# Hybrid mLSTM / latent-attention encoder layer: weight buffers that change roles, projection operands built during attention, an earlier last column

## Chip, cores and metric

One core of one Trainium2 chip runs the whole program in one launch. The metric is the device time of one execution in microseconds (us). The median of three runs of the kernel before is 1942.12 us (1938.83 to 1942.77).

## What is computed

One encoder layer is applied to two token groups of 512 tokens (`x_prompt`, `x_sample`; width 1024) with shared fp32 weights:

```python
u = h @ w_in                                   # h = rmsnorm(x); q,k,v,o, gates, c_q, c_kv, k_r, gm
hm = rmsnorm(mlstm(q, k, v, log_i, log_f))     # both directions, 4 heads
y_m = (sigmoid(o) * hm) @ w_mo
y_a = mla_attention(q_nope, q_rope, k_nope, k_rope, va) @ w_ao     # 8 heads
g_m, g_a = split(sigmoid(gm), 2)
x = x + (g_m * y_m + g_a * y_a) @ w_out
h2 = rmsnorm(x)
x = x + (silu(h2 @ w_gate) * (h2 @ w_up)) @ w_down                 # 2816 wide
x = x + sigmoid(x @ w_ple_gate) * (p @ w_ple)
y = rmsnorm(x)
```

## The kernel before

**Tiles and precision.** Activations are kept feature-major: a tile is 128 features by the 512 tokens of one group g. Every operand of a product is split into a high and a low fp32r part: a cast on ScalarE (ACT) makes the high part (`xh`, `wp`, `whi`), a subtraction on VectorE (DVE) the low part (`xl`, `wp`, `wlo`), and three matmuls hi·hi, hi·lo, lo·hi accumulate in PSUM.

**Order of the work.** A scheduler orders the instructions of each engine; the stretches between `pinned[0] = True` and `pinned[0] = False` (embedding projection, last column and tail) keep the program's order. All DMAs are issued in order by one queue engine (SP); a DMA waits there for its buffer to be free, and all later ones behind it. The stages, with their place in the profiled execution:

| stage | us | code |
|---|---|---|
| mLSTM, 4 heads | 30 to 600 | `mlstm_proj` (L464), `mlstm_chain` (L529) |
| attention, 8 heads, 16 half-heads (head `hd`, group g) | 600 to 871 | loop at L950 |
| merged projections `w_mo`, then `w_ao` | 871 to 1031 | `Seven`, `chain` (L840, L891) |
| output projection, embedding projection `emb` | 1031 to 1166 | L1076 |
| feed-forward gate and up, 22 units | 1166 to 1600 | `Seven`, `chain` |
| down projection | 1590 to 1830 | `Seven`, `chain` |
| ple gate, final norm, outputs | 1830 to 1938 | L1286 to L1299 |

**Seven products.** `Seven` computes a 2x2 block product (two groups, two blocks of weight columns) with seven products instead of eight, as in Strassen's scheme. One unit needs the four weight blocks a11, a12, a21, a22, which come in two loads of 512 KB: the first (a11|a12) into a buffer `wst` of pool WP, the second (a21|a22) into a buffer `wst` of pool WX; each pool has two such buffers. POOL adds and subtracts weight blocks in place, ACT and DVE split them into `wp` tiles (`wsplit`), PE multiplies. `chain` interleaves units: the order is P6(i), P1(i+1), P5(i), P2(i+1), Q4(i), P7(i+1), P3(i). So a11 and a12 are needed first (P1, P2) and come free last (P3, split in the last place), and a21, a22 come free two products earlier (Q4).

**Activation operands.** `Ops` builds the seven operands of each of the four feature blocks k from four tiles a, b (group 0 and 1, block k) and c, d (block k + 4): P1 = a, P2 = c, P3 = d, P7 = b − d, P6 = P7 − a, P5 = a − b, Q4 = P6 + c. Each is split into an `xh`/`xl` pair in pool H (P1, P2, P7, P6: 32 tiles) or OP. For `w_mo` the tiles come from the DRAM scratch `hzd`, which `mlstm_chain` wrote (L602 to L603: (tanh + 1)·hm). `hraw` loads a tile into X2, a pool opened at head 7, and multiplies it by the head-norm gain `hg` on ACT. All of P1, P2, P7 (`hops.need`) is asked for at head 7, ahead of that head's two half-heads; P6 comes with `chain`'s look-ahead.

**Embedding and tail.** `emb` (L1076) splits the weights `wple` in the step that uses them first. At the end, `finish` writes normalised output columns of a half of group 1 on DVE, `embed` computes the last embedding column with its squares, `sums` and `inv` the norm.

All instructions of the kernel before are recorded through one wrapper, so every row of its profile has line L77; groups are told apart by the tiles' names. Names in what follows: `ld` a loaded activation tile, `t` a difference of such tiles, `hn` a normalised activation tile, `sc`, `p`, `pt`, `aph`/`apl`, `av` the scores, probabilities, their transposes, their split and the attention output, `b` the PSUM bank of a `Seven` product, `mm` one of the other projections, `actd` the DRAM copies of feed-forward activations.

## Time and profile before

| quantity | value |
|---|---|
| median of 3 runs | 1942.12 us |
| profiled execution, its own time | 1939.74 us |
| span of the profiled execution | 1938.0 us |
| PE busy | 1861.9 us (96%), 8836 instructions |
| DVE busy | 1260.3 us (65%), 2135 instructions |
| ACT busy | 874.7 us (45%), 1711 instructions |
| POOL busy | 474.4 us (24%), 349 instructions |
| mean granted TensorE clock | 0.981 |

PE is TensorE's matmul stream. Busy time of PE holds the waits inside a running chain of matmuls only in part, so a stretch is better judged by its count of matmuls against the count of a stretch that is known to be full. "Granted clock" is 1.00 at 2.4 GHz and 0.50 at 1.2 GHz.

### The profile page before, as it was taken

The numbers are of one execution on the slowest core, as the hardware profiler recorded it, in microseconds if no ns is written. First come the engines' busy times: TensorE is split into PE (matmuls) and PEld (weight loads), VectorE is DVE, ScalarE is ACT, GpSimd is POOL, SyncE is SP. The second block draws the span as 40 slices with busy tenths as digits, with TensorE's granted clock in tenths as the row PEclk, the third lists the DMA queues.
The fourth block names the chain that finished last, engine by engine and source line by source line (L and its number), as shares of the span: only waits on it lengthen the run. The fifth ranks groups of instructions, "written<-read, shape, count | busy, mean of one in ns | idle before, by whom it ended". The sixth has DMA issues, their size and how long they took to land. (4 is left out here: it accounts for less than half of the span.)

```text
span 1938.0 us, 24531 instructions
## 1 busy us (share of the span) xinstructions
PE 1861.9 (96%) x8836; PEld 1542.6 (80%) x8836; DVE 1260.3 (65%) x2135; ACT 874.7 (45%) x1711; POOL 474.4 (24%) x349
## 2 busy tenths in 40 slices
PE   7999999999999999979899989999999999999997
PEld 6888898988888888758777867777887777788886
DVE  7657575746455676878996667445444458778757
ACT  5245454535354566784533435233333344434442
POOL 3000000100000001234630014565466654232100
PEclk9999999999999999989999989999999999999998
DMA  4110112012262122137554331233223346534232
GB/s 161 50 44 33 55 35 64 34 60 82 82 202 90 55 74 73 53 115 239 163 200 153 109 114 66 87 111 106 94 97 102 115 135 218 163 120 142 87 125 87
DMA packets 95578, 203.40 MB, mean 105 GB/s; under 512 B 10400, under 2 KB 21024, under 8 KB 95456
## 3 DMA queue, kind: packets, MB, share of 16 engines
q1 hardware_dynamic: 95456, 201.83, 31.2%
q8 instruction: 69, 1.13, 0.2%
q14 instruction: 53, 0.43, 0.1%
HBM read 147.69 MB, written 54.10 MB: 104 GB/s over the span
## 5 line engine op out<-in xcount | busy, mean ns | idle before, releaser
L77 PE MATMUL b<-xh,wp 128*128 128x512 f32 x2296 | 723.4, 396 | 17.9 <-ACT wp L77 8.3
L77 PEld LDWEIGHTS b<-xh,wp 128*128 128x128 f32 x2296 | 434.5, 190 | 124.4 <-ACT wp L77 11.7
L77 PE MATMUL b<-xl,wp 128*128 128x512 f32 x1148 | 452.4, 394 | 5.9 <-DVE xl L77 5.7
L77 DVE TENSOR_TENSOR wp<-wst,wp 128x512 fp32r<-128x512 f32 (+1 forms) x284 | 271.9, 964 | 108.8 <-ACT wp L77 108.0
L77 ACT CAST wp<-wst 128x512 fp32r<-128x512 f32 (+1 forms) x284 | 171.0, 611 | 345.4 <-PE b L77 228.1
L77 PEld LDWEIGHTS b<-xl,wp 128*128 128x128 f32 x1148 | 217.8, 190 | 54.3 <-DVE xl L77 7.6
L77 PE MATMUL mm<-hh,whi 128*128 128x512 f32 x592 | 233.1, 394 | 7.2 <-ACT whi L77 7.0
L77 PE MATMUL mm<-hh,wlo 128*128 128x512 f32 x592 | 232.4, 394 | 2.2 <-DVE wlo L77 2.2
L77 PE MATMUL mm<-hl,whi 128*128 128x512 f32 x592 | 233.0, 394 | 1.1 <-DVE hl L77 1.1
L77 POOL TENSOR_TENSOR s<-wst,wst 128x512 f32<-128x512 f32 (+1 forms) x42 | 61.6, 1466 | 449.5 <-DMA wst<-w 323.4
L77 PEld LDWEIGHTS mm<-hh,whi 128*128 128x128 f32 x592 | 112.2, 190 | 30.6 <-ACT whi L77 7.0
L77 POOL TENSOR_TENSOR wst<-wst 128x512 f32<-128x512 f32 (+1 forms) x84 | 125.7, 1496 | 35.3 <-DVE wp L77 30.7
L77 PEld LDWEIGHTS mm<-hh,wlo 128*128 128x128 f32 x592 | 112.1, 189 | 26.1 <-DVE wlo L77 3.4
L77 PEld LDWEIGHTS mm<-hl,whi 128*128 128x128 f32 x592 | 112.1, 189 | 25.5 <-DVE hl L77 2.3
L77 DVE TENSOR_TENSOR u<-b,u 128x512 f32<-128x512 f32 x90 | 61.3, 687 | 107.6 <-PE b L77 82.7
L77 ACT CAST whi<-wst 128x1024 fp32r<-128x1024 f32 (+1 forms) x71 | 73.1, 1029 | 110.4 <-PE mm L77 77.6
L77 DVE TENSOR_TENSOR wlo<-wst,whi 128x1024 fp32r<-128x1024 f32 (+1 forms) x71 | 86.0, 1211 | 28.7 <-ACT whi L77 28.3
L77 POOL TENSOR_TENSOR vnl<-avt,vnh 128x512 fp32r<-128x512 f32 x16 | 21.5, 1345 | 317.6 <-ACT vnh L77 284.6
L77 DVE TENSOR_TENSOR xl<-ld,xh 128x512 fp32r<-128x512 f32 x109 | 88.7, 846 | 8.1 <-ACT xh L77 7.8
L77 PE MATMUL mm<-xh,wp 128*128 128x512 f32 (+1 forms) x288 | 81.7, 368 | 0.0
L77 ACT COPY u<-b 128x512 f32<-128x512 f32 x90 | 50.9, 586 | 66.6 <-PE b L77 65.6
L77 DVE TENSOR_TENSOR x<-x,b 128x512 f32<-128x512 f32 x84 | 56.9, 682 | 32.8 <-PE b L77 32.4
(269 smaller groups left out, 3379.4 us busy)
## 6 DMA issues: line engine op xcount, KB each, us to landing
wst<-w SPq DMA_DIRECT2D x135, 512.0 KB
ld<-actd SPq DMA_DIRECT2D x77, 256.0 KB
actd<-t SPq DMA_DIRECT2D x44, 256.0 KB
actd<-sg SPq DMA_DIRECT2D x33, 256.0 KB
x<-x SPq DMA_DIRECT2D x32, 256.0 KB
wst<-wd SPq DMA_DIRECT2D x16, 512.0 KB
hzd<-hz SPq DMA_DIRECT2D x16, 256.0 KB
tmd<-tg SPq DMA_DIRECT2D x16, 256.0 KB
```

Source lines behind the costliest of these rows:

```text
L77: r = f(*args, **kw)
```

## The change

Five edits, each with its own place:

- **A.** `mlstm_proj` multiplies and shifts the tanh tile by `hg` on ACT (`hg`·tanh + `hg`, 16 more ACT instructions of 128x512), so that `hzd` already holds the gained product; in the chain the DVE operation is a plain product. The 16 multiplications by `hg` in `hraw` go.
- **B.** The 16 units of operands P1, P2, P7, P6 of `w_mo` are asked for in the six half-heads (4,0) to (6,1), 3, 3, 3, 3, 2 and 2 units each (`HOPS`). Their tiles pass through four staging buffers (two `rs` of H, two `bk` of EV), and P7 and P6 are made in place of b. At head 7 the 16 tiles are loaded a second time into X2 for P5, Q4, P3; there Q4 = (c − a') − d with a' = a − b takes two subtractions on POOL for each block instead of one addition.
- **C.** `Seven` gives the first load a WP buffer and the second a WX buffer in two units, and the other way round in the next two.
- **D.** `emb` splits the weights of the next step one step ahead.
- **E.** The last `embed` and its sums of squares (now without the DVE addition, in eight instead of four small matmuls) go ahead of outputs 2 and 3, and outputs 4 to 7 are spread among the norm's steps.

```diff
@@ mlstm_proj
                 S.activation(out=to[g][c], in_=to[g][c], func=AF.Tanh, scale=0.5)
+                hc = hg[:, 2 * hd + c : 2 * hd + c + 1]
+                S.activation(out=to[g][c], in_=to[g][c], func=AF.Identity, scale=hc, bias=hc)
@@ mlstm_chain
-            V.scalar_tensor_tensor(out=zt, in0=to[g][c], scalar=1.0, in1=tp, op0=ALU.add, op1=ALU.mult)
+            V.tensor_tensor(out=zt, in0=to[g][c], in1=tp, op=ALU.mult)
@@ Ops.part
             if name == "P7":
-                t = self.t[k] = self.tmp()
+                t = self.t[k] = self.tmp() or self.get("b", k)
...
-            else:
+            elif k in self.t:
                 t = self.t[k]
                 add(out=t, in0=t, in1=self.get("c", k), op=ALU.add)
+            else:
+                t = self.get("c", k)
+                add(out=t, in0=t, in1=self.get("a", k), op=ALU.subtract)
+                add(out=t, in0=t, in1=self.get("d", k), op=ALU.subtract)
@@ Seven
-            for sl, src in zip((WP, WX), srcs):
+            for sl, src in zip((WP, WX) if wsn[0] % 4 < 2 else (WX, WP), srcs):
...
+            wsn[0] += 1
@@
+    stage = [(H, "rs"), (H, "rs"), (EV, "bk"), (EV, "bk")]
+    raws = [0]
+
     def hraw(g, k):
-        t = load(hzd[g][k], X2, "x")
-        S.activation(out=t, in_=t, func=AF.Copy, scale=hg[:, k : k + 1])
-        return t
-
-    tmps = [(H, "rs"), (H, "rs"), (EV, "bk"), (EV, "bk")]
-    hops = Ops(hraw, lambda: (lambda s: s[0](s[1], "t"))(tmps.pop(0)), lambda n: V if n == "P7" else GP)
+        raws[0] += 1
+        return load(hzd[g][k], *stage[raws[0] % 4])
+
+    hops = Ops(hraw, None, lambda n: V if n == "P7" else GP)
+    hops.tmp = lambda: None
+    units = [(n, [k]) for k in range(4) for n in ("P1", "P2", "P7", "P6")]
@@ attention loop
             X2 = Slots("X2", "right", x=16)
-            for n in ("P1", "P2", "P7"):
-                hops.need(n)
+            hops.r, hops.t = {}, {}
+            hops.raw = lambda g, k: load(hzd[g][k], X2, "x")
         for g in range(G):
             attn(hd, g, ops[g])
             if hd < AH - 1:
                 ops[g] = attn_proj(hd + 1, g, wa)
+            for _ in range(HOPS.get((hd, g), 0)):
+                hops.need(*units.pop(0))
@@ emb
-            if c // 2 == len(wple):
+            while len(wple) < min(4, c // 2 + 2):
@@ tail
-    finish(1, [0, 1, 2, 3], 0, H0)
-    embed(KD - 1, 1, bk[3], toks[1], bps[1])
+    first = rs2[1]
+    finish(1, [0, 1], 0, H0)
+    embed(KD - 1, 1, bk[3], toks[1], bps[1], True)
+    finish(1, [2, 3], 0, H0)
     sums(1, H0, H0)
     inv(1, H0)
-    rs_ = rs2[1]
+    finish(1, [4, 5], 0, H0)
     spread3(1, H0, H0)
...
+HOPS = {(4, 0): 3, (4, 1): 3, (5, 0): 3, (5, 1): 3, (6, 0): 2, (6, 1): 2}
```

**Where instructions move.** First, the DMA issues of SP in the feed-forward stage, for one unit: `wst` is a weight load (the lower number is the first, a11|a12), `actd<-t` a store of an activation. Before:

```order
L849 DMA wst_13171<-w 128x1024
L1134 DMA actd_13030<-t_13014 128x512
L1134 DMA actd_13026<-t_13015 128x512
L849 DMA wst_13169<-w 128x1024
L1134 DMA actd_13028<-t_13016 128x512
L1134 DMA actd_13032<-t_13017 128x512
```

and now:

```order
L855 DMA wst_13201<-w 128x1024
L1150 DMA actd_13062<-t_13046 128x512
L1150 DMA actd_13058<-t_13047 128x512
L855 DMA wst_13203<-w 128x1024
L1150 DMA actd_13060<-t_13048 128x512
L1150 DMA actd_13064<-t_13049 128x512
```

Before, the second load (13171) stood ahead of the first (13169); now the first (13201) stands ahead, in the place that comes free with Q4 of an earlier unit, and the second (13203) behind it.

Second, VectorE in attention around half-head (4,0): `mx` rows are steps of the softmax, `apl` is the low part of the transposed probabilities, `qnl` of a query, `wp_8554` a weight of the merged projection's first unit. Before:

```order
L77 RECIPROCAL mx_7378<-mx_7378 128x1
L77 TENSOR_SCALAR mx_7398<-mx_7398 128x1
L77 TENSOR_TENSOR apl_7331<-pt_7365,aph_7330 128x4x128
L77 TENSOR_REDUCE mx_7464<-sc_7458 128x1
L77 RECIPROCAL mx_7398<-mx_7398 128x1
L77 TENSOR_TENSOR qnl_7437<-pj_7428,qnh_7435 128x512
L77 TENSOR_SCALAR mx_7464<-mx_7464 128x1
L77 TENSOR_TENSOR wp_8554<-s_1510_8551,wp_8554 128x512
L77 TENSOR_REDUCE mx_7484<-sc_7478 128x1
```

and now:

```order
L152 TENSOR_TENSOR xl_7622<-ld_7484,xh_7620 128x512
L152 TENSOR_TENSOR xl_7628<-ld_7624,xh_7626 128x512
L752 RECIPROCAL mx_7394<-mx_7394 128x1
L152 TENSOR_TENSOR xl_7634<-ld_7630,xh_7632 128x512
L752 RECIPROCAL mx_7414<-mx_7414 128x1
L748 TENSOR_REDUCE mx_7501<-sc_7495 128x1
L152 TENSOR_TENSOR qnl_7453<-pj_7444,qnh_7451 128x512
L748 TENSOR_REDUCE mx_7521<-sc_7515 128x1
L805 TENSOR_TENSOR ld_7789<-ld_7789,ld_7791 128x512
```

Before, all `xl` rows of these operands stood in and behind head 7. Now all 16 pairs and the four P7 subtractions (20 DVE rows) lie between the softmax rows of half-heads (3,1) and (5,0); (6,1), (7,0) and (7,1) have none. `ld_7789` takes the staging buffer of `ld_7484`, whose last reader on DVE is the first row, eight rows ahead.

Third, VectorE at the end of the embedding projection, where the normalised tiles `hn` and the operands `xl` of the feed-forward stage are made. Before:

```order
L77 TENSOR_TENSOR wp_10725<-wst_10560,wp_10725 128x512
L77 SCALAR_TENSOR_TENSOR hn_10748<-x_1855_10275,cols,rbc_10720 128x512
L77 SCALAR_TENSOR_TENSOR hn_10750<-x_1912_10493,cols,rbc_10720 128x512
L77 TENSOR_TENSOR wp_11000<-wst_10974,wp_11000 128x512
L77 TENSOR_TENSOR t_10762<-hn_10748,hn_10750 128x512
L77 TENSOR_TENSOR xl_10766<-t_10762,xh_10764 128x512
L77 SCALAR_TENSOR_TENSOR hn_10778<-x_1870_10334,cols,rbc_10720 128x512
L77 SCALAR_TENSOR_TENSOR hn_10780<-x_1924_10542,cols,rbc_10720 128x512
L77 TENSOR_TENSOR t_10762<-t_10762,hn_10377 128x512
L77 TENSOR_TENSOR wp_10782<-wst_10561,wp_10782 128x512
```

and now:

```order
L79 TENSOR_TENSOR wp_10760<-wst_10593,wp_10760 128x512
L79 SCALAR_TENSOR_TENSOR hn_10783<-x_1867_10307,cols,rbc_10755 128x512
L79 SCALAR_TENSOR_TENSOR hn_10785<-x_1924_10525,cols,rbc_10755 128x512
L152 TENSOR_TENSOR wp_11010<-wst_11006,wp_11010 128x512
L152 TENSOR_TENSOR wp_11032<-wst_11006,wp_11032 128x512
L79 TENSOR_TENSOR t_10797<-hn_10783,hn_10785 128x512
L79 TENSOR_TENSOR xl_10801<-t_10797,xh_10799 128x512
L79 SCALAR_TENSOR_TENSOR hn_10813<-x_1882_10366,cols,rbc_10755 128x512
```

The split of the third weight block, which stood behind four `hn` and `t` rows (wp_10782 from wst_10561), now stands ahead of the first `hn` row (wp_10760 from wst_10593).

## Rows read from the trace of the kernel before

**Rows 1.** Windows view of full stretches: bounds, length, PE, PEld, DVE, ACT, POOL busy (count), clock, DMA, GB/s

```profile
100.00:640.00 540.00, 539.65 (x3020) 472.31 (x3019) 320.10 (x697) 258.17 (x603) 21.23 (x33) 1.00 0.21 71
...
1705.00:1820.00 115.00, 115.00 (x505) 94.50 (x505) 88.90 (x133) 46.00 (x82) 31.06 (x24) 1.00 0.38 122
```

**Rows 2.** Windows view in attention: half-heads (3,1) to (5,0), and the last half-head

```profile
755.45:800.43 44.98, 43.58 (x217) 35.20 (x216) 36.23 (x80) 34.09 (x72) 10.39 (x8) 1.00 0.16 54
...
838.41:871.56 33.15, 18.80 (x66) 13.24 (x65) 25.21 (x42) 26.80 (x53) 12.01 (x9) 0.74 0.20 68
```

**Rows 3.** What PE waited for, 838.41 to 871.56: us in total, times, longest

```profile
PE sc L77 <- ACT p L77: 8.5, 3, 3.6
PE pt L77 <- DVE apl L77: 2.5, 2, 1.4
PE av L77 <- DVE apl L77: 2.1, 1, 2.1
```

**Rows 4.** Groups of ACT, 838.41 to 871.56: busy us, mean ns, idle before

```profile
L77 ACT ACTIVATE ld<-ld,hg 128x512 f32<-128x512 f32 x13 | 9.3, 754 | 0.0
L77 ACT CAST xh<-t 128x512 fp32r<-128x512 f32 x8 | 4.9, 620 | 5.2 <-POOL t L77 5.2
...
L77 ACT CAST xh<-ld 128x512 fp32r<-128x512 f32 x7 | 4.3, 651 | 0.0
```

**Rows 5.** Groups of DVE, 838.41 to 871.56

```profile
L77 DVE TENSOR_TENSOR xl<-t,xh 128x512 fp32r<-128x512 f32 x8 | 8.5, 1084 | 2.4 <-ACT xh L77 2.3
L77 DVE TENSOR_TENSOR xl<-ld,xh 128x512 fp32r<-128x512 f32 x8 | 5.8, 740 | 1.4 <-ACT xh L77 1.3
...
L77 DVE TENSOR_TENSOR t<-ld,ld 128x512 f32<-128x512 f32 x4 | 2.8, 692 | 1.0 <-ACT ld L77 1.0
```

**Rows 6.** The chain that ended last: start, us, a step at 1611

```profile
1611.19 3.22 DMA ld<-actd
```

**Rows 7.** Windows view in the feed-forward and down stages

```profile
1225.00:1240.00 15.00, 12.58 (x48) 9.57 (x47) 5.27 (x5) 3.39 (x6) 7.81 (x6) 0.89 0.28 88
1240.00:1580.00 340.00, 336.24 (x1455) 271.65 (x1454) 165.59 (x182) 117.72 (x209) 192.33 (x129) 1.00 0.30 99
1580.00:1600.00 20.00, 18.24 (x72) 14.25 (x71) 12.93 (x16) 9.94 (x20) 10.46 (x7) 0.91 0.71 233
1624.00:1645.00 21.00, 16.52 (x63) 12.84 (x62) 13.97 (x21) 7.46 (x13) 11.58 (x7) 0.84 0.82 298
1690.00:1705.00 15.00, 13.39 (x51) 10.31 (x50) 11.74 (x16) 7.35 (x13) 5.80 (x4) 0.89 0.45 140
```

**Rows 8.** Timeline of SP and ACT in the feed-forward stage

```profile
1301.67 0.33 SPq L849 DMA_DIRECT2D wst<-w  x1
...
1306.33 0.33 SPq L849 DMA_DIRECT2D wst<-w  x1
...
1310.59 1.14 ACT L77 CAST wp<-wst 128x512 fp32r<-128x512 f32 x2 [5.42 <-DMA wst<-w]
```

**Rows 9.** What PE waited for, 1240 to 1580

```profile
PE b L77 <- DVE wp L77: 2.2, 8, 0.5
```

**Rows 10.** Timeline of ACT at the start of the down projection

```profile
1630.54 0.62 ACT L77 CAST xh<-ld 128x512 fp32r<-128x512 f32 x1 [8.54 <-DMA ld<-actd]
```

**Rows 11.** Windows view at the end of the embedding projection

```profile
1138.00:1166.00 28.00, 21.89 (x72) 16.13 (x73) 23.56 (x33) 15.32 (x29) 10.12 (x7) 0.82 0.39 141
1166.00:1186.00 20.00, 18.38 (x79) 14.20 (x78) 20.00 (x23) 12.80 (x23) 10.83 (x7) 1.00 0.11 35
```

**Rows 12.** What PE waited for, 1138 to 1166

```profile
PE mm L77 <- ACT wp L77: 3.8, 3, 2.3
PE mm L77 <- DVE wp L77: 2.4, 2, 1.3
```

**Rows 13.** Timeline of DVE and PE in the tail: start, us, engine, instruction, wait

```profile
1923.56 1.65 DVE L77 SCALAR_TENSOR_TENSOR o<-x,cols,rbc 128x256 f32<-128x256 f32 x4
...
1926.48 0.42 DVE L77 TENSOR_TENSOR sq<-sq,sq 128x256 f32<-128x256 f32 x1 [0.48 <-ACT sq L77]
...
1927.05 0.98 PE L77 MATMUL ssc<-onesr,sq 128*128 128x2 f32 x4 [3.69 <-DVE sq L77]
...
1928.07 0.16 DVE L77 TENSOR_SCALAR rv<-ssc 128x4 f32<-128x4 f32 x1 [1.17 <-PE ssc L77]
```

More of the change, by code (lines that the diff above doesn't have):

```diff
@@ L74, in __getattr__ @@
             f = getattr(self.e, name)
+            if not pinned[0]:
+                return f
             def call(*args, **kw):
                 r = f(*args, **kw)
-                if pinned[0]:
-                    tc.keep_in_program_order(r)
+                tc.keep_in_program_order(r)
                 return r
@@ L824, in need @@
                     x.append((hi, lo))
-    wpn = [0]
+    wpn, wsn = [0], [0]
     def wpair():
@@ L903, in chain, with make @@
         made = {}
+        def make(i):
+            if i not in made:
+                made[i] = quads[i][1]()
         for at, (q, n) in enumerate(order):
@@ L906, in chain @@
                 quads[i][0].need(m)
-            for i, m in order[at : at + 2]:
-                if i not in made:
-                    made[i] = quads[i][1]()
+            for i, _ in order[at : at + 2]:
+                make(i)
             made[q].product(n)
@@ L1288, in encoder_kernel @@
     spread3(1, 0, H0)
-    finish(1, [0, 1, 2, 3], 0, H0)
-    embed(KD - 1, 1, bk[3], toks[1], bps[1])
+    first = rs2[1]
+    finish(1, [0, 1], 0, H0)
+    embed(KD - 1, 1, bk[3], toks[1], bps[1], True)
+    finish(1, [2, 3], 0, H0)
     sums(1, H0, H0)
     inv(1, H0)
-    rs_ = rs2[1]
+    finish(1, [4, 5], 0, H0)
     spread3(1, H0, H0)
-    rs2[1], rs_ = rs_, rs2[1]
-    finish(1, [4, 5, 6, 7], 0, H0)
-    rs2[1] = rs_
+    rs2[1], second = first, rs2[1]
+    finish(1, [6, 7], 0, H0)
+    rs2[1] = second
     finish(1, list(range(KD)), H0, H0)
```

## The prediction

> **What bounds the kernel now.** I read the window view first, because PE's 96% says little: inside a running chain, waits can hide in the busy time. A stretch that is known to be full gives the measure. From 1705 to 1820 us 505 matmuls of 128x512 take 115.00 us [rows 1], so one costs 0.228 us and 4.39 go into a microsecond. A stretch's matmul count divided by 4.39, taken from its length, is what PE lost there. By that measure the mLSTM is full (539.65 of 540.00 us busy, clock 1.00 [rows 1]), and the losses lie in a few places: the last attention half-head (66 matmuls in 33.15 us [rows 2]), the end of the embedding projection, four short places in feed-forward and down, and the tail. After the window view I read the waits of PE in those places, then the groups of the engine named there, and at last the timeline around one wait. The reader is to see in each who is late, and whether the change touches that one. The granted clock falls with each pause (0.74, 0.82, 0.84 and 0.89 in the windows with losses [rows 2, 7, 11]), so a pause that goes gives back more than its own length; the counts hold this already.
>
> **A, gain applied in the mLSTM.** 16 ACT operations at about 0.75 us [rows 4] are 12 us more on an engine that is busy 258.17 of 540.00 us while PE is never short [rows 1]. The cover is that half of ACT which is idle. One wait of a product tile for its tanh could show: 0, at most +1 us. At head 7 the 13 rows `ld<-ld,hg` of that window go (9.3 us [rows 4]); that is counted under B.
>
> **B, operands built earlier.** Two places change with opposite sign.
>
> *The gain, 838.41 to 871.56.* PE waits three times, 8.5 us in all, for a softmax `p` of ACT [rows 3], and ACT's queue there is full of operand work: 9.3 us scaling, 4.9 and 4.3 us casts [rows 4], together 18.5 of 26.80 us busy. All of that leaves. The 66 matmuls need 15.0 us at full pace, so at most 18 us can come back. The softmax's own chain stays (the `apl` waits, 2.5 and 2.1 us [rows 3], partly). I take 8.5 for the `p` waits and 3.5 of the 4.9 that the clock costs (18.80 us busy at 0.74 instead of 1.00): **−12** (−8 to −14).
>
> *The price, 755.45 to 800.43.* Here, by the order of rows, all 16 pairs now stand. DVE is busy 36.23 of 44.98 us [rows 2] and gets 20 more operations of about 0.69 us [rows 5], 13.8 us: 50.0 in a stretch of 45, hence +5 at least if nothing else gives way. PE has nothing to give: it is busy 43.58 of 44.98. To this comes POOL, which now does the four P6 subtractions there: `xl` took 740 ns in one group and 1084 in another, beside POOL's work on `t` [rows 5]; 20 times 0.344 would be 6.9 us, I take 4. ACT has 34.09 busy and gets 16 casts of 0.63, 10 us: 44, just full. On SP the 16 loads go through four buffers, and one landing takes 3.2 us [rows 6]; the eight DVE rows between a buffer's last reader and its next use are worth 4.5 us (44.98 us over 80 rows, eight times), so most landings are covered; 1 to 2 us for those that are not. Sum: **+11**, between +4 (attention's slack elsewhere absorbs DVE's surplus) and +16 (nothing is absorbed). Behind a late load on SP stands an `avt` load of a later half-head, and behind a late `xl` on DVE the softmax maxima that PE's next transposes need.
>
> The 16 second loads at head 7 (256 KB each) and the four further POOL subtractions serve P5, Q4 and P3, which come after three products of the first unit; DMA is at 0.20 there [rows 2]: nothing. B is then **−1**, from −10 to +8.
>
> The row of 740 against 1084 ns bears on a rule. The Trainium skill, page "SBUF — State Buffer", section "Who interferes with whom", says that a DVE instruction with two SBUF inputs and a GpSimd instruction that reads SBUF lock each other out for the whole instruction. It speaks against putting twenty such subtractions beside POOL's. By it every microsecond of POOL in the stretch, 10.39 and about 7 more, could stand in front of DVE, and B would be about +12 instead of −1, the total near 1935; the rows show a stretching of 344 ns and not a whole POOL instruction, so the sum goes by the rows.
>
> **C, weight buffers.** In feed-forward a unit's first load is issued behind its second, at 1306.33 and 1301.67 us, because its buffer comes free later; ACT's cast of the first block then waits 5.42 us for it [rows 8] and PE for the subtraction behind the cast, eight times, 0.5 us at most [rows 9]. In the new order the first load stands in the earlier place, 4.7 us ahead. That is more than any of these waits. Lost by counts: 1225 to 1240: 65.9 − 48 matmuls, 4.1 us; 1580 to 1600: 87.8 − 72, 3.6; 1690 to 1705: 65.9 − 51, 3.4 [rows 7]; and of the 8.7 us of 1240 to 1580 (1493 − 1455) those of the eight waits, 2.2 idle and, as I assume, half as much again for the slower matmuls behind each pause, 3.4. Sum 14.5. Not touched is 1624 to 1645 (92.2 − 63, 6.6 us): there the weight's cast stands on ACT behind an `xh` cast that waits 8.54 us for an `actd` load [rows 10], and the order of those rows is unchanged; PE that arrives earlier waits longer there. I give 2.5 back for that: **−12**, between −15 and −6 (the three stops have other causes in part, DMA being at 0.71 in one [rows 7]).
>
> **D, weights of the embedding projection a step ahead.** 1138 to 1166 holds 72 of 123 matmuls: 11.6 us lost, 6.2 of them waits for `wp` [rows 12]. These go. But DVE is busy 23.56 of 28.00 and then 20.00 of 20.00 us [rows 11], and the feed-forward stage cannot start faster than its `hn`, `t` and `xl` rows on DVE. Only the 4.4 us of DVE's idle time can be won, and about 1 more from the clock: **−5.5** (−9 to −3).
>
> **E, tail.** Before the norm's first step on DVE (`rv`, 1928.07) stand four output rows (1.65 us for four, 0.41 each) and the addition of squares (0.42, ahead of it 0.48 idle), and PE's `ssc` waits 3.69 us for it [rows 13]. Two outputs (0.8) and the addition (0.57 with its start) leave the path; four more small matmuls are 0.98 for four at the clock there, some of it overlapped, and outputs 4 to 7 fill the waits of the norm. **−1.4** (−2 to −0.7).
>
> **Sum**, against the profiled execution's 1939.74 us: 0 − 1 − 12 − 5.5 − 1.4 = −20, so 1920. The median of the runs, 1942.12, lies 2.4 above the profiled execution; the forecast of the median is **1922 us**.
>
> **Rivals.** A measurement of this kernel tells about 0.2%, 3.9 us, from no change.
> - *VectorE decides in attention.* DVE stays saturated past the stretch, none of its surplus is absorbed, and the clock drops at the pauses as it does in the other stretches. For it: 50 us of work in 45. Against it: the gains elsewhere don't hang on it. B's price is then +16 and 2 to 3 of clock, the total −13: about 1930. The rule of the skill above, at 1935, is the far end of this case. Chance 0.18.
> - *The earlier weight load wins nothing.* POOL's additions and the `actd` loads set the pace, and C's 14.5 us turn into other waits. For it: POOL is busy 192.33 of 340.00 us in feed-forward [rows 7] and the stop at 1624 has that form. Against it: the waits named are on `wp`, whose chain begins with the load [rows 8, 9]. The total is −8: 1934. Chance 0.10.
> - *Both together*, which is no change: −20 + 7 + 12, about 1941. Chance 0.07.
> - *The staging ring serialises, slower.* If the DVE rows between a buffer's last reader and its next use take less than a landing's 3.2 us [rows 6], each of the 16 loads stands bare in front of a cast or a subtraction, and the softmax queues behind it on ACT and DVE. 16 times 3.2 is 51 us on top of 36.23 of DVE [rows 2]: the stretch goes from 45 to 87 us, +42; with −12, −12, −5.5 and −1.4 that is +11: 1953. It decides if a landing under contention (DMA is at 0.16 here, at 0.82 elsewhere [rows 2, 7]) outlasts the eight rows. Chance 0.08.
>
> **How the numbers follow.** The forecast gets 0.57. Its own bounds, not all at one end together, give 1909 to 1933. The range takes in the first two rivals with their spread: 1906 to 1937; left out are the ring, no change and the outer tails, some 0.18. Faster by over 0.2% (below 1938.2): the forecast, the first rival but for 0.01 and most of the second, 0.82. Within 0.2%: the rest of these and most of "both", 0.09. Slower: the ring and a tail of "both", 0.09.
>
> **What the profile after would show.** C: no `b` waiting for DVE `wp` in feed-forward, and the stops from 1225 to 1240, 1580 to 1600 and 1690 to 1705 gone; if instead POOL's sums or `ld<-actd` are named there, C was wrong. D: no `mm` waiting for `wp`, DVE with no gap up to the start of feed-forward, and a stretch 4 to 7 us shorter. B: no `p` waits of 3 us in the last half-head, which takes about 21 us instead of 33; and around half-head (4,0) to (4,1) DVE close to 100% with PE waits for `mx`, `apl` or `p` adding to about 11 us. The ring would show as `xh` casts on ACT with 2 to 3 us of waiting for `ld<-hzd`, many times. E: `rv` about 1.4 us nearer to the last embedding product. A total above 1938 with the stops of feed-forward gone would mean that attention's price was missed; one above 1938 with them still there, that the load's place was not their cause. Below 1906 the price in attention would have been near nothing.

## The result, and the profile after

The changed kernel takes **1916.22 us** (median of 4 runs, 1915.40 to 1917.75) against 1942.44 us for the kernel before beside it (4 runs, 1938.83 to 1943.34): 26.2 us less, ratio 0.9869 (95% interval 0.9852 to 0.9886). The profiled execution took 1915.43 us, its span is 1913.7 us, 24.3 less than before. Forecast were 1922 us, 20 us less on the profiled execution.

The page after, its first part:

```profile
span 1913.7 us, 24573 instructions
PE 1848.8 (97%) x8840; PEld 1538.4 (80%) x8840; DVE 1236.9 (65%) x2134; ACT 881.0 (46%) x1711; POOL 476.6 (25%) x353
```

PE's busy time fell by 13.1 us with four matmuls more, and its mean granted clock rose from 0.981 to 0.988: slow matmuls at a reduced clock are part of what went, waits inside running chains may be another.

Where the time went is read best from the start of one and the same matmul in both timelines. The k-th matmul of a kind (`nm<-va,pl`, `av<-apl,vnh`, `b<-xl,wp` and so on) can be looked up in both. PE's order did change, from 158 us on: the scheduler set many matmuls elsewhere. But as many matmuls stand ahead of each mark of the next table in one kernel as in the other (3922, 4417, 5486, 5853 and 8370), so its stretches hold equal work.

| from one mark to the next | mark, before | mark, after | change in this stretch | forecast |
|---|---|---|---|---|
| start to the last merge-gate matmul | 748.35 | 747.18 | −1.2 | 0 (A) |
| to the first merged product | 871.60 | 864.53 | −5.9 | −1 (B) |
| to the last matmul of the output projection | 1129.82 | 1122.91 | +0.2 | 0 |
| to the 309th `b<-xl,wp`, early in feed-forward | 1226.44 | 1216.52 | −3.0 | −5.5 (D) |
| to the last `b<-xl,wp`, end of the down projection | 1830.08 | 1807.24 | −12.9 | −12 (C) |
| to the end of the span | 1938.0 | 1913.7 | −1.5 | −1.4 (E) |

The first line is not the change's: see the last section.

**Attention.** The `av<-apl,vnh` matmuls, 64 in all, show both halves of B. Ahead of the 45th and the 53rd stand 15 and 9 matmuls more than in the old order; at the other four the counts agree.

| matmul | before | after | difference |
|---|---|---|---|
| 29th | 752.91 | 751.74 | −1.17 |
| 33rd | 770.61 | 774.18 | +3.57 |
| 45th | 810.81 | 822.42 | +11.61 |
| 53rd | 834.36 | 846.60 | +12.24 |
| 57th | 856.12 | 855.07 | −1.05 |
| 64th | 871.13 | 864.08 | −7.05 |

From the 29th to the 53rd 13.4 us are lost, from there to the first merged product 19.3 won. Of both, some 1.5 us are order: five score matmuls (0.228 us each) and four transposes (128x128, four in 0.35 us) moved from behind the 53rd to ahead of it. For equal work the loss is 11.9 us and the gain 17.8. In the window view of the profile after, columns as in [rows 1]:

```profile
749.90:800.00 50.10, 43.19 (x198) 33.79 (x197) 45.77 (x92) 39.70 (x82) 15.09 (x11) 0.97 0.47 145
800.00:834.00 34.00, 32.07 (x154) 26.36 (x153) 27.90 (x62) 25.91 (x53) 6.64 (x5) 0.95 0.16 47
834.00:864.00 30.00, 26.75 (x133) 20.57 (x132) 19.09 (x43) 21.24 (x44) 18.12 (x15) 1.00 0.56 202
```

DVE is busy 45.77 of 50.10 us where the operands are built, and PE does 198 matmuls there; the last half-head, which lost 18 us by the forecast's count [rows 2], runs at clock 1.00 here (0.94 in the second profile of this kernel). What PE waited for from 749.9 to 834 us, and then from 834 to 864.5:

```profile
PE pj L181 <- DVE mx L749: 2.8, 1, 2.8
PE sc L742 <- ACT p L751: 2.4, 2, 1.9
PE pj L181 <- DVE rs L695: 1.4, 1, 1.4
PE pt L759 <- DVE mx L749: 1.1, 1, 1.1
```

```profile
PE sc L742 <- ACT p L751: 1.3, 1, 1.3
PE pt L759 <- DVE apl L152: 1.2, 2, 0.9
```

These answer to [rows 3]: the `p` waits of the last half-head fell from 8.5 to 1.3 us, and in the stretch before DVE's softmax rows (`mx`) and projections (`rs`) are late instead.

**Feed-forward.** The windows that answer to [rows 7]:

```profile
1215.00:1230.00 15.00, 15.00 (x68) 12.33 (x67) 5.57 (x7) 4.50 (x8) 7.22 (x6) 1.00 0.12 44
1240.00:1560.00 320.00, 318.39 (x1387) 259.62 (x1386) 145.13 (x172) 111.97 (x195) 186.54 (x125) 1.00 0.30 101
1560.00:1580.00 20.00, 20.00 (x89) 16.41 (x88) 15.09 (x19) 13.19 (x26) 11.35 (x8) 1.00 0.80 266
1602.00:1625.00 23.00, 17.80 (x67) 14.07 (x66) 13.46 (x21) 7.52 (x14) 10.54 (x7) 0.85 0.75 264
1665.00:1680.00 15.00, 15.00 (x67) 12.27 (x66) 13.91 (x19) 7.91 (x14) 5.83 (x4) 1.00 0.57 178
```

Three of the stops are full stretches now (68, 89 and 67 matmuls where 65.9, 87.8 and 65.9 are full pace). The stop that the forecast left alone is still there: 67 matmuls in 23 us, clock 0.85. One unit in SP's and ACT's timelines shows why [rows 8] changed:

```profile
1286.61 1.01 SPq L855 DMA_DIRECT2D wst<-w  x1
...
1291.27 0.33 SPq L855 DMA_DIRECT2D wst<-w  x1
```

```profile
1291.56 0.63 ACT L843 CAST wp<-wst 128x512 fp32r<-128x512 f32 x1 [1.45 <-DMA wst<-w]
```

The first load is issued 4.7 us ahead of the second, as forecast, and the cast waits 1.45 us for it instead of 5.42. The forecast called 4.7 us more than any of these waits; that holds for PE's (0.5), not for ACT's 5.42, of which a part is left. From 1240 to 1565 PE's waits for DVE's `wp` [rows 9] are gone; one row is left:

```profile
PE b L894 <- ACT u L929: 1.6, 6, 0.3
```

**Before feed-forward.** The windows that answer to [rows 11]:

```profile
1128.00:1147.30 19.30, 19.26 (x89) 15.73 (x87) 16.28 (x25) 9.24 (x17) 9.08 (x6) 1.00 0.52 187
1147.30:1166.00 18.70, 8.88 (x32) 7.14 (x33) 17.78 (x26) 11.75 (x22) 8.85 (x3) 0.73 0.19 71
```

The embedding projection is full now, its last matmul starts 19.1 us earlier than before, 12.2 of them won in the projection itself. Ten of the 19.1 go at once, in one pause before the first feed-forward product, which starts 9.1 us earlier than before (PE's timeline):

```profile
1157.12 0.79 PE L894 MATMUL b<-xh,wp 128*128 128x512 f32 x1 [9.86 <-ACT em L79]
```

**Tail.** The rows that answer to [rows 13]:

```profile
1902.90 0.83 PE L79 MATMUL ssc<-onesr,sq 128*128 128x2 f32 x6 [1.58 <-ACT sq L79]
1903.76 0.16 DVE L79 TENSOR_SCALAR rv<-ssc 128x4 f32<-128x4 f32 x1 [0.59 <-PE ssc L79]
```

From the end of the last embedding product to `rv` it is 3.7 us (1900.11 to 1903.76), before 5.2 (1922.92 to 1928.07).

### The profile page after: what moved, and what is told of

The parts are those of the page before. It is cut to its first block, busy times and chain, and to the rows that moved or that the text cites. A ratio compares the mean times of both kernels' runs of the same rounds, so it can differ in the third digit from the quotient of the medians.

```text
span 1913.7 us, 24573 instructions
## 1 busy us (share of the span) xinstructions
PE 1848.8 (97%) x8840; PEld 1538.4 (80%) x8840; DVE 1236.9 (65%) x2134; ACT 881.0 (46%) x1711; POOL 476.6 (25%) x353
## 4 chain that ended last, share of the span: by engine, by line
PE 82%; DVE 9%; DMA 3%; issue 2%; ACT 2%; POOL 1%; SPq 0%; DVEq 0%; ACTq 0%; POOLq 0%
PE b L894 12%; PE b L896 11%; PE b L895 11%; PE mm L181 8%; PE mm L183 8%; PE mm L182 8%; PE nm L580 3%; PE mm L79 2%; PE mm L495 2%; PE mm L497 2%; PE mm L496 2%; DVE xl L152 2%; DVE wp L152 1%; PE mm L1236 1%; PE mm L1235 1%
## 5 line engine op out<-in xcount | busy, mean ns | idle before, releaser
L894 PE MATMUL b<-xh,wp 128*128 128x512 f32 x1148 | 444.1, 395 | 20.6 <-ACT em L79 9.9
L896 PE MATMUL b<-xh,wp 128*128 128x512 f32 x1148 | 445.8, 393 | 1.2 <-DVE wp L152 1.0
L843 ACT CAST wp<-wst 128x512 fp32r<-128x512 f32 (+1 forms) x271 | 164.5, 611 | 328.2 <-PE b L896 270.7
L152 DVE TENSOR_TENSOR wp<-wst,wp 128x512 fp32r<-128x512 f32 (+1 forms) x271 | 246.0, 910 | 92.5 <-ACT wp L843 92.5
L894 PEld LDWEIGHTS b<-xh,wp 128*128 128x128 f32 x1148 | 217.2, 189 | 73.5 <-ACT em L79 10.3
L183 PEld LDWEIGHTS mm<-hh,wlo 128*128 128x128 f32 x592 | 112.2, 190 | 26.5 <-DVE wlo L152 3.4
L152 DVE TENSOR_TENSOR xl<-ld,xh 128x512 fp32r<-128x512 f32 x121 | 96.1, 826 | 10.9 <-ACT xh L1169 5.9
L152 DVE TENSOR_TENSOR wlo<-wst,whi 128x1024 fp32r<-128x1024 f32 (+1 forms) x70 | 86.4, 1235 | 24.9 <-ACT whi L166 24.7
```

The source lines that it names most:

```text
L152: e.tensor_tensor(out=out, in0=src, in1=hi.bitcast(F32), op=ALU.subtract)
L183: last_mm[0] = E.matmul(bk, wlo[:, c], hi, start=False, stop=k == nk - 1)
L843: S.copy(hi, src)
L894: E.matmul(bk, whi[:, c], hi, start=bool(first) and k == 0, stop=False, **sk)
L896: E.matmul(bk, wlo[:, c], hi, start=False, stop=k == self.kh - 1, **sk)
```

## The experiments

### One part alone

**C alone**, and C with the roles changed at every unit:

```diff
-            for sl, src in zip((WP, WX), srcs):
+            for sl, src in zip((WP, WX) if wsn[0] % 4 < 2 else (WX, WP), srcs):
...
+            for sl, src in zip((WP, WX) if wsn[0] % 2 < 1 else (WX, WP), srcs):
```

> The kernel before with C alone (weight buffers change roles every two units). From the trace after, the feed-forward and down stages account for 12.9 us of the whole 24.3. Theory: the buffer's role alone makes it, because the first load of a unit is issued some 4.7 us earlier. Then this kernel takes 12 to 14 us less than before, about 1929, and the eight waits of PE for DVE's wp in feed-forward (2.2 us) are gone. Rival: C needs the later start that B and D give PE, or gives back what it wins in the down stage when it stands alone; then it takes 4 to 8 us less, 1934 to 1938.

Measured: 1927.92 us against 1940.67 (ratio 0.9941, 0.9921 to 0.9961), 12.7 less. In PE's timeline the stretch from the 309th to the last `b<-xl,wp` is 12.4 us shorter, and from 1240 to 1580 us PE has no wait for `wp`. C needs no other part for it.

> As C alone, but the buffers change roles at every unit instead of every two. Theory: the gain comes from the first load taking a buffer that a second load two units ago held. With two buffers in each pool and a change at every unit, the first load of unit i again takes the buffer of the first load of unit i-2, which comes free last: no gain, within 4 us of before (1938 to 1946), and PE's waits for wp are as before. Rival: any mixing of the pools spreads the loads and helps; then 6 to 13 us less than before.

Measured: 1940.70 against 1940.67, ratio 0.9998 (0.9987 to 1.0008). The waits, from 1240 to 1580 us, are those of before [rows 9] to the digit:

```profile
PE b L894 <- DVE wp L152: 2.2, 8, 0.5
```

So the gain does not come from spreading loads over two pools, but from whose buffer the first load takes: only with the period of two units is it one that comes free at Q4.

**A and B alone, D alone** (the other hunks of the diff taken back):

> The kernel before with A and B alone (gain applied in the mLSTM, operands built in six half-heads). By the traces, matmuls from the end of the merge gates to the first merged product take 5.9 us less: 12.2 us lost between 752 and 834 us, 19.3 won between 834 and 871 and 1.2 earlier. Theory: this is B's own, so this kernel takes 5 to 7 us less than before, about 1936.5, and shows the same loss and gain. Rival: the merged projections give it back when C's loads are not there (their units use the same buffers): under 2 us less.

Measured: 1932.61 against 1940.67 (0.9963, 0.9950 to 0.9976), 8.1 less by the medians. In its trace the stretch from the last merge-gate matmul to the first merged product is 3.9 us shorter than before; its 53rd `av` starts 14.9 us later than that of before, where the changed kernel's is 12.2 later. It gains 2.7 more from the 309th to the 337th `b<-xl,wp`, where before had a stop; C alone gains 4.6 in the same place. The loss and the gain belong to A and B; the size differs by some 2 us between two profiles.

> The kernel before with D alone (weights of the embedding projection split a step ahead). By the traces the projection itself ends 12.2 us earlier, and 9 us of that go in one pause of 9.85 us before the first feed-forward product. Theory: the pause does not depend on the rest of the change; this kernel takes 2 to 4.5 us less than before, about 1939, and has a pause of 8 to 11 us there. Rival: the pause comes from DMA or from C's new order of loads; then the pause is under 4 us and the gain 8 to 12 us, about 1932.

Measured: 1936.48 against 1940.67 (0.9983, 0.9973 to 0.9994), 4.2 less. The embedding projection ends 12.65 us earlier, the 309th `b<-xl,wp` is reached 2.9 earlier (0.65 of each were won ahead of the first merged product, where nothing was changed), and the pause is there:

```profile
1164.22 0.80 PE L892 MATMUL b<-xh,wp 128*128 128x512 f32 x1 [10.52 <-ACT em L79]
```

12.7 + 8.1 + 4.2 is 25.0; with E's 1.5 it is 26.5, and the whole change made 26.2. The parts add up within their errors: each ratio is uncertain by 2 to 4 us, and the 2.7 us that A and B win at a stop which C removes as well are counted twice. E was not run alone. In the kernels without it (before, both of C, A and B, D alone) it is 15.0 to 15.5 us from the last `mm<-xl,wp` to the end of the span; in those with it 13.9 to 14.6, so E made between 0.4 and 1.6.

### What holds the pause before feed-forward

```diff
-        emb(1)
+        emb(min(3, len(todo)))
         h2.need("P7", [k])
-        emb(1)
```

> The changed kernel, but in the embedding projection's last part three projection steps (with their ACT copies em) are written ahead of each P7 operand instead of one ahead and one behind. Nothing is left out. In the trace after, PE stands for 9.85 us between the last matmul of this projection and the first of feed-forward, although that first product's operands are long made; ACT's copies em, which free the PSUM banks, stand behind a cast xh<-t that waits for DVE's t. Theory 1 (banks): the copies hold the pause; with them ahead of the casts the pause falls under 2 us, and 6 to 10 us come off the whole, about 1908. Theory 2 (my forecast's reason: DVE's operand rows themselves bound the start): the pause moves behind the first two or four products, to P7 or P6, and under 3 us are won: 1913 to 1917.

Measured: 1914.31 us, ratio to before 0.9875 (0.9853 to 0.9897), the changed kernel's own being 0.9869: no gain. The pause is gone, and three others have come behind it (PE's timeline):

```profile
1163.41 0.50 PE L896 MATMUL b<-xh,wp 128*128 128x512 f32 x1 [1.65 <-DVE wp L152]
1168.48 0.80 PE L895 MATMUL b<-xl,wp 128*128 128x512 f32 x1 [2.09 <-DVE xl L152]
1174.24 0.80 PE L896 MATMUL b<-xh,wp 128*128 128x512 f32 x1 [3.68 <-DVE wp L152]
```

The window from the end of the projection, first of the changed kernel and then of this one:

```profile
1147.30:1176.00 28.70, 18.88 (x76) 15.43 (x77) 26.25 (x36) 19.23 (x35) 14.96 (x7) 0.82 0.15 55
```

```profile
1147.30:1176.00 28.70, 21.28 (x79) 15.85 (x78) 28.70 (x40) 17.65 (x31) 12.53 (x7) 0.80 0.13 47
```

76 matmuls or 79 in the same 28.7 us, with DVE busy 28.70 of 28.70. The wait that the trace names in the changed kernel (ACT's copies `em`, which stand behind casts that wait for DVE) is real but stands in for the bound: DVE's operand rows, busy 26.25 of 28.70 us in the changed kernel. Theory 2 holds.

### What A does for B

```diff
-                S.activation(out=to[g][c], in_=to[g][c], func=AF.Identity, scale=hc, bias=hc)
...
+        S.activation(out=t, in_=t, func=AF.Copy, scale=hg[:, k : k + 1])
```

The last line stands behind the staging load and behind the second load at head 7; in the mLSTM the DVE operation of before is back.

> The changed kernel with A undone: the gain is not applied in the mLSTM but on ACT to each staged tile (16 more ACT operations of 0.75 us between half-heads (3,1) and (5,0)) and again after the second load at head 7 (16 more). Theory: A is what makes room for B; ACT is busy 33.96 of 43.50 us there and the scaling stands between a load and its cast, so the stretch grows by 4 to 10 us and the second scaling at head 7 costs 0 to 4: 4 to 12 us slower than the changed kernel, 1920 to 1928. Rival: DVE alone bounds the stretch and ACT's added work is hidden; then within 3 us of the changed kernel.

Measured: 1928.43, ratio 0.9945 (0.9926 to 0.9965), about 12 to 15 us slower than the changed kernel, and for the larger part not in the place that I named. Up to the 53rd `av` it is within 3 us of the changed kernel and ends there 0.7 behind; from the 53rd to the 57th it loses 10.3. But ten score matmuls, 2.3 us, come later than the 53rd here and earlier in the changed kernel: for equal work it loses some 2.5 us up to the 53rd and 8.1 behind it. The groups of ACT from 840 to 876 us, and two of PE's waits there, show what stands there:

```profile
L977 ACT ACTIVATE ld<-ld,hg 128x512 f32<-128x512 f32 x16 | 10.9, 736 | 0.0
L759 ACT CAST aph<-pt 128x512 fp32r<-128x512 f32 x11 | 6.5, 593 | 0.9 <-PE pt L757 0.9
```

```profile
PE pt L757 <- ACT p L752: 3.3, 3, 2.6
PE pt L757 <- DVE apl L152: 1.2, 2, 0.9
```

The scaling hides for the most part in the DVE-bound stretch (ACT rises to 45.49 of 50.10 us from 749.9 to 800 us), but in the last half-heads 10.9 us of it on ACT cost PE 8.1 us. From the last merge-gate matmul to the first merged product this kernel takes 128.0 us, the changed one 117.4, the kernel before 123.3: without A, B loses 4.8 us there instead of winning 5.9.

### What the price in attention is made of

The low parts of some staged operands moved from DVE to POOL (8: those of P7 and P6; 16: all):

```diff
-                    lo_of(lo, src, hi)
+                    lo_of(lo, src, hi, self.lo(name))
...
+    hops.lo = lambda n: GP if n in ("P7", "P6") else V
```

> The changed kernel with the low parts of P7 and P6 (8 subtractions) made on POOL instead of DVE in attention. Theory 1 (DVE's work decides): 8 times 0.69, 5.5 us less on DVE, so 2 to 5 us faster, 1911 to 1914. Theory 2 (the skill's rule on two-input subtractions beside POOL's reads of SBUF): each POOL instruction of 1.3 to 1.7 us that overlaps DVE's rows stretches them, and 8 of them take back what DVE saves: within 2 us, or up to 5 slower.

Measured: 1913.61, ratio 0.9868 (0.9847 to 0.9889), in the medians not to be told from the changed kernel. In the trace the stretch from the last merge-gate matmul to the first merged product is 2.7 us shorter than the changed kernel's, with DVE 3 us less busy:

```profile
749.90:800.00 50.10, 44.21 (x201) 34.55 (x199) 42.79 (x87) 40.48 (x83) 26.34 (x19) 0.97 0.48 152
```

> The changed kernel with all 16 low parts of the staged operands on POOL, twice the dose of the run with 8 (there DVE's busy time in 50.1 us fell from 45.77 to 42.79, and the half-head behind it was reached 2.5 us earlier). Theory 1 (DVE's work decides): 11 us less on DVE, 3 to 7 us faster than the changed kernel. Theory 2 (POOL becomes the bound, or locks DVE out): POOL gets 16 times 1.38 = 22 us on top of 15 in 50; DVE's rows with two operands in SBUF grow from 0.75 to over 1 us, and the gain of 8 is lost again: within 2 us of the changed kernel, or slower.

Measured: 1918.59 against 1917.71 for the changed kernel beside it; the stretch is 0.9 us shorter than the changed kernel's. DVE fell to 40.38 us and PE did not gain (200 matmuls):

```profile
749.90:800.00 50.10, 43.41 (x200) 33.90 (x198) 40.38 (x74) 38.23 (x78) 34.78 (x26) 0.97 0.51 160
```

Four P7 subtractions of DVE grew from 688 ns (changed kernel) to 1224:

```profile
L806 DVE TENSOR_TENSOR ld<-ld,ld 128x512 f32<-128x512 f32 x4 | 4.9, 1224 | 1.2 <-DMA ld<-hzd 1.2
```

So twice the dose gives a third of the gain of 8; DVE's sum of work is not the whole price. The next runs move nothing between engines. They hold all rows of a unit (ACT's casts, DVE's and POOL's subtractions) in program order and so spread them otherwise:

```diff
+                pinned[0] = True
                 hops.need(*units.pop(0))
+                pinned[0] = False
...
-HOPS = {(4, 0): 3, (4, 1): 3, (5, 0): 3, (5, 1): 3, (6, 0): 2, (6, 1): 2}
+HOPS = {(4, 0): 6, (4, 1): 4, (5, 0): 4, (5, 1): 2}
```

First with `HOPS` left as it is (rows from (4,1) to (7,0)):

> The changed kernel with the operand rows of the 16 units held in program order, so that they lie from half-head (4,1) to (7,0) instead of (3,1) to (5,0); the same instructions. Theory 1 (DVE's sum of work decides the price): 20 rows of 0.69 us spread over six half-heads, where DVE has 2 to 4 us free in each, are hidden more: the loss from 752 to 834 us falls from 12 to between 2 and 6 us, the gain behind it stays, and the whole is 5 to 9 us faster: about 1909. Theory 2 (each load through four buffers stands bare, wherever it is): the same loss, only later; within 3 us of the changed kernel, or slower because rows held in order wait for their loads and keep the softmax behind them.

Measured: 1919.35, ratio 0.9895 (0.9873 to 0.9918): 2 to 5 us slower than the changed kernel, by its two medians and ratios, and the intervals overlap. In the trace the stretch from the last merge-gate matmul to the first merged product is 2.5 us longer. At the 56th `av` it is 4.8 us ahead (both counted from the last merge-gate matmul), but with ten score matmuls and four transposes not yet done, 2.6 us of work: the lead is some 2.1 us, and of the 7.3 us that it loses from there to the last some 4.6 are left. Softmax rows wait there again:

```profile
PE pt L759 <- ACT p L754: 2.8, 2, 2.3
PE pt L759 <- DVE apl L152: 1.2, 1, 1.2
```

Then with the units asked for earlier:

> The changed kernel with the operand rows held in program order and asked for in 6, 4, 4, 2 units from half-head (4,0) to (5,1), so that by the order of rows they lie from (4,1) to (6,0), with nothing behind (6,1). Held in order to (7,0) they won 4.8 us up to half-head (7,0) and lost 7.3 in the last one and a half. Theory 1 (the price is DVE's sum of work, the gain needs an empty queue in the last half-heads): the first is kept in part, the second is not lost: 2 to 5 us faster than the changed kernel. Theory 2 (rows held in order make the softmax wait wherever they stand): no faster, or up to 5 slower.

Measured: **1912.38 us** (4 runs, 1911.20 to 1913.42), the changed kernel beside it 1917.71 (1913.83 to 1918.44): 5.3 us faster, and faster than either kernel. Ratio to before 0.9857 (0.9839 to 0.9875). By the traces 3.3 us of this (3.4 against the second profile of the changed kernel) lie between the last merge-gate matmul and the first merged product. Another 2.1 us between this profile and that second one lie ahead of the gate, where the two kernels do not differ (see the last section). DVE's work is the same, PE's is not: windows 749.9 to 834 us, first of the changed kernel, then of this one:

```profile
749.90:834.00 84.10, 75.27 (x351) 60.15 (x350) 73.67 (x152) 65.61 (x134) 21.73 (x16) 0.96 0.34 106
```

```profile
749.90:834.00 84.10, 77.09 (x366) 60.41 (x365) 74.37 (x156) 65.98 (x137) 21.69 (x16) 1.00 0.36 108
```

351 matmuls become 366 beside the same DVE rows. The windows begin at slightly different matmuls, and the second profile of the changed kernel has 357; the measure for equal work is from the 29th to the 53rd `av`, 397 matmuls in each: 91.5 us here, 94.9 and 93.4 in the two profiles of the changed kernel. Where the rows stand decides with their sum.

> As the last, with 4, 4, 4, 4 units and the 8 low parts of P7 and P6 on POOL. Theory 1 (DVE's sum of work): 2 to 3 us faster than the kernel held in order with all low parts on DVE, 4 to 8 faster than the changed kernel. Theory 2 (POOL's instructions stretch DVE's, or waits of rows held in order): no faster than that kernel.

Measured: 1913.99 (0.9867, 0.9849 to 0.9885), 3.7 faster than the changed kernel beside it and 1.6 slower than the last kernel. Its attention is the shortest of all (4.4 us less than the changed kernel's), but its start was late by 3.8 us in this profile. Whether it is better than the last kernel stays open.

> The changed kernel once more, as the measure for the other three on the same chip, and to see which differences between two profiles of one program are noise: 1913 to 1919 by both theories; the first 100 us, where no instruction was changed, may differ by 1 to 3 us.

Measured: 1917.71 us, ratio 0.9879 (0.9855 to 0.9903): the same kernel as the 1916.22 above. From the last merge-gate matmul to the first merged product it differs by 0.1 us from the first profile of it, from there to the last matmul by 0.7, but up to that gate by 2.7.

## Why the prediction was right, point by point

The forecast of 1922 us was 6 us too high, in its range (1906 to 1937) and on its side; the sum of −20 was −24.3 in the profile. That it came so close is in part luck: B was 4.9 us better than forecast and D 2.5 worse, and 1.2 us of the rest were won ahead of attention, where nothing of the change shows.

- **C** (−12; measured −12.9, alone −12.7). The mechanism, the 4.7 us and the three stops came as written. Given back were 1.1 us at the first down product, where 2.5 were allowed: the cast that PE waits for still stands behind an `xh` cast that waits for an `actd` load (8.68 us, before 8.54), and PE's wait for it is now 5.2 us, before 4.5. The rival "the earlier weight load wins nothing" fell: POOL is busy 186.54 of 320.00 us there, and PE loses 4.1 us (1405 matmuls at full pace, 1387 done) where it lost 8.7 of 340. That is 4.6 less, where 3.4 were booked; but the half that I added for slower matmuls behind each pause was not the clock, which is 1.00 in that window before and after, so that not every pause lowered it.
- **B's price** (+11, +4 to +16; measured 13.4 in the first profile, 12.0 in the second, from the 29th to the 53rd `av`; 11.9 and 10.4 for equal work). DVE was 91% busy, where close to 100% was forecast; PE's six waits from 749.9 to 834 us sum to 8.9 us, and waits for loads on DVE were 1.6 us against 1 to 2. The term for POOL (4 us) was too high in the changed kernel: 16 `xl` took 749 ns each, nearly the 740 of [rows 5]. Order is a part of the price: held in program order and early, the same rows lose 2 to 3 us less for equal work.
- **B's gain** (−12, −8 to −14; measured −19.3, and −17.8 for equal work) is the step that failed: its size, not its mechanism. I let the softmax's own chain stay, `apl` waits included [rows 3], and let the clock come back by three quarters. The 17.8 us are nearly the 18 that I had given as the most, and even that bound was too low: 24 of the 66 matmuls are transposes of 128x128, of which four take 0.35 us, so the 66 need some 11.7 us at full pace and not 15.0, and 21.4 were lost. From the 53rd `av` to the first merged product, by the same working, 21.9 us were lost before and 4.0 are lost now. The `apl` waits fell from 4.6 to 1.2 us, and to 1.4 in the run without A, where ACT stays loaded and DVE's 16 `xl` rows of 14.3 us [rows 5] are gone from the queue: most of them stood behind those rows and were no latency of the softmax. The clock was 0.74 before and is 1.00 and 0.94 in the two profiles now. The run without A shows the ACT side alone: 10.9 us of scaling cost 8.1.
- **D** (−5.5, −9 to −3; measured −3.0, alone −4.2 by the medians, with an interval of 1 to 5). The reason was right, DVE's rows bound the start of feed-forward, and the run with the copies ahead shows it. The size was too large: I counted 4.4 us of idle DVE time as winnable and added a microsecond for the clock; after the change DVE is busy 16.28 of 19.30 and 17.78 of 18.70 us, and the clock falls in the new pause (0.73).
- **E** (−1.4; measured −1.5, by other pairs of kernels 0.4 to 1.6) and **A** (0) came as written: from the 17th `mm<-hl,whi` to the last merge-gate matmul the kernels without A take 720.9 to 722.5 us, those with it 720.9 to 722.7 and one 724.1, and the longer ones differ from the shorter by drops of the clock (last section).
- **The rivals.** VectorE does decide in attention, but the clock, which was to cost 2 to 3 us more, stayed at 0.95 to 0.97 (1.00 in the second profile), and the gain behind it was larger. The ring that would serialise did not: in all of 749.9 to 793.4 us DVE waited 1.6 us for `ld<-hzd`, and ACT's `xh` casts, which the forecast had named as the sign, waited 1.4 us for it, once.
- **The rule that speaks against B.** The Trainium skill, page "SBUF — State Buffer", section "Who interferes with whom", would have made B cost 12 us by the bound that I drew from it, which took all of POOL's time as lost to DVE. In the changed kernel the `xl` rows took 749 ns. (The section says that such a pair contends and that the lock is exclusive; "for the whole instruction" stands there of DVE's two-port modes.) But the trace agrees with the rule where such a row does meet POOL. In the changed kernel POOL runs weight additions from 1144.23 to 1150.56 us, and DVE's rows with two SBUF operands beside them (1.5 to 1.8 us) are more than twice as long as those behind (0.68):

```profile
1146.00 1.78 DVE L152 TENSOR_TENSOR wp<-wst,wp 128x512 fp32r<-128x512 f32 x1
1147.70 1.74 DVE L79 TENSOR_TENSOR t<-hn,hn 128x512 f32<-128x512 f32 x1
1149.37 1.75 DVE L811 TENSOR_TENSOR hn<-hn,hn 128x512 f32<-128x512 f32 x1
1151.04 0.68 DVE L79 TENSOR_TENSOR xl<-t,xh 128x512 fp32r<-128x512 f32 x1
```

```profile
1145.60 1.62 POOL L870 TENSOR_TENSOR wst<-wst 128x512 f32<-128x512 f32 x1
1147.31 1.59 POOL L872 TENSOR_TENSOR wst<-wst,wst 128x512 f32<-128x512 f32 x1
1148.97 1.59 POOL L879 TENSOR_TENSOR wst<-wst 128x512 f32<-128x512 f32 x1
```

  Each DVE row lasts about as long as POOL's instruction beside it. At 0.68 us each, these three and the `t` row ahead of them (1.52) would take 4.1 us less, in the very place where DVE bounds the start of feed-forward; no run moved POOL's additions away, so what that is worth stays open. In attention few such rows meet POOL: from 749.9 to 800 us two of the `xl` rows overlap one of its instructions and take 0.90 and 1.56 us, the others 0.66 to 0.69. A row that reads PSUM, as `mx<-sc`, keeps its 0.68 us beside POOL:

```profile
760.24 0.68 DVE L748 TENSOR_REDUCE mx<-sc 128x1 f32<-128x512 f32 x1
785.95 1.56 DVE L152 TENSOR_TENSOR xl<-ld,xh 128x512 fp32r<-128x512 f32 x1
```

```profile
759.46 1.98 POOL L152 TENSOR_TENSOR vnl<-avt,vnh 128x512 fp32r<-128x512 f32 x1
785.68 1.28 POOL L869 TENSOR_TENSOR s<-wst,wst 128x512 f32<-128x512 f32 x1 [4.19 <-DMA wst<-w]
```

  With 16 more POOL instructions the P7 rows grew to 1224 ns. So in this kernel the bound is to be counted over those DVE rows alone that have two operands in SBUF and meet a POOL instruction.

## What to carry to other kernels

When operand work leaves a queue in front of a latency chain, count every row that leaves, on all engines, and ask whether the chain's own waits are made of the same queue: here most of its `apl` waits went with the rows, and four fifths of the stretch's loss came back. Look at where a buffer comes from, not at how many there are: an order of roles with the right period put a load 4.7 us earlier, and one with the wrong period did nothing. When the trace names a wait, look at whether the engine behind it is full: removing the named wait in front of a full VectorE moved the pause and won nothing. And when two kernels are compared from one matmul to another, count the matmuls between them: nine that the scheduler moved made 1.5 us of loss in one stretch and of gain in the next. Count them by kind, too: a transpose of 128x128 is not a matmul of 128x512.

## What was not expected of the hardware

Equal instructions differ from execution to execution in their first thirty microseconds: the start of the 17th `mm<-hl,whi` lies at 27.45 us in the kernel before, at 24.77 in the changed one, and at 27.16 in the second profile of the changed one, while the eleven other profiles lie between 24.9 and 28.6; no instruction was changed there. The window from 18 to 22 us shows what differs, the granted clock (before, then the changed kernel):

```profile
18.00:22.00 4.00, 3.38 (x8) 2.70 (x9) 4.00 (x7) 2.74 (x5) 0.10 (x1) 0.50 0.55 167
```

```profile
18.00:22.00 4.00, 3.52 (x15) 2.93 (x16) 4.00 (x7) 2.88 (x6) 0.25 (x1) 1.00 0.52 164
```

The clock goes from its lower level, 1.2 GHz, to 2.4 GHz earlier in one execution than in another. It also falls in some executions alone: from 424 to 426 us it is 0.50 in the changed kernel and 1.00 in the kernel before, and 1.6 us are lost there. The second profile of the changed kernel, D alone and the run with 16 low parts on POOL lose them too, so this does not come from A. The early rise and this drop make all but 0.1 of the 1.2 us ahead of the gate: 2.7 won in the first 25 us, 1.6 lost at 425. Of the 24.3 us between the two profiled spans some 1 to 3 can be such luck, and differences under 3 us between two profiles are only to be read between marks that lie close together.
